# Down-projection of a conv-FFN layer with its operand sums on VectorE, output work in smaller pieces over more steps, samples' sums copied out at its start, and TensorE's last feature tile written in program order

## The chip, the cores and the metric

One core of a Trainium2 chip (trn2). The metric is the device time of one execution in microseconds (us). The kernel before took 1695.22 us, the median of three runs (1693.51 to 1695.83).

## What is computed

One layer of a chunk-causal streaming encoder on a prompt of 1024 rows and 8 sample sequences of 16 rows, all in float32. Token mixing (attention and spatial gating) comes first; the change touches only the second half, the channel mixing:

```python
D_MODEL = 1024; SEQ = 1024; DEC_BATCH = 8; DEC_SEQ = 16; CONV_W = 3; D_FF = 2816

def conv_ffn(h, conv_cache, w_ffn_in, ffn_conv_w, ffn_conv_b, w_ffn_out):
    g, u = jnp.split(h @ w_ffn_in, 2, axis=-1)
    gp = jnp.concatenate([conv_cache, g], axis=1)
    gc = ffn_conv_b
    for j in range(CONV_W):
        gc = gc + ffn_conv_w[j] * gp[:, j:j + T]
    out = (jax.nn.gelu(gc) * u) @ w_ffn_out
    return out, gp[:, -(CONV_W - 1):]

x = x + gt2 * conv_ffn(h2, ...)[0]      # gt2: a gate, one row for the prompt, one for each sample
```

The last two rows of gp of every sequence are outputs as well (the conv rows).

## The kernel before

A float32 matrix product is made of three matmuls: each operand is split into a rounded part and the rest (`split`, lines 77 and 78: ScalarE, called ACT, copies the rounded part, VectorE, called DVE, subtracts it), and rounded x rounded, rounded x rest and rest x rounded are added up in PSUM. Large products are made by Strassen's scheme, seven products of half-size blocks in place of eight; their operands are blocks (A11, A12, A22 and so on) and sums of blocks (S1 to S4 of the activations, T1 to T4 of the weights).

**Feature tiles (lines 1074 to 1337, loop at 1542).** The 2816 features are 22 tiles, f = 0 to 21. Of each, `up_weights` loads four blocks of w_ffn_in (SyncE, called SP, issues the loads), GpSimd (POOL) makes t3, t1, t2 and t4 out of them (lines 1093, 1094, 1098, 1102), and ACT and DVE split them into wB11, wB21, wT2, wT1, wT3, wT4, wB22. `unit(f, u)` makes the tile in two halves, u = 0 and 1, each of seven products (`product`, matmul at line 1225) of twelve matmuls, 128 x 288 each: X takes A11, then S2 with T2, S3 with T3 and A22 with T4; Y takes A12; Z takes S1 with T1 and S4 with B22. Between its products X is copied out by ACT: x1c at line 1301, u2 at 1315 (after T2), u3 at 1321 (after T3), and the last at 1331. The next product into X waits for the copy. Convolution, GELU and gate follow on ACT and DVE, and `gated` stores the gated tile to DRAM (aT_d, line 1269). `sample_down(f, hf)` does the samples' part of the down-projection at once: three matmuls (line 1283) add to acc_s, two PSUM banks held from f = 0 to the end. It also makes sums of w_ffn_out blocks on POOL and stores them for later.

**Down-projection (`down`, line 1375, and its inner functions).** Seven products (j = 0 to 6, `KINDS`) of eleven steps k, 77 steps n. A step is twelve matmuls, 128 x 512 each (`multiply`, line 1495), into four banks dX or dZ. `prepare(j, k)` runs three steps ahead: it loads the blocks of activations (`load_a`, line 1394, tiles named ar) and of weights (`get`, line 1406; dB, dT and, for T3, a second one dT3y), makes a sum of two (T3 at 1422, S1 at 1429, S2 at 1431, S3 at 1433, S4 at 1435) and splits both into da and dw. `finish` takes a full bank out, and `delay(n, ...)` puts its further work (add to another bank's, times the gate g2p, plus x1, store) some steps later. `scaled` (line 1453) loads the x1 rows and does the gate's product and the sum on POOL. `samples_out` (line 1499) reads acc_s at step 9, `conv_rows` (line 1355) at step 10 transposes the conv rows on PE (glt, line 1359), copies them (glo, DVE, line 1361) and stores them in five pieces (SP, lines 1365 to 1369). The gates are loaded at steps 1 and 2 (g2p, line 1522) and 1 to 8 (g2s, 16 small loads, line 1526).

**What sets the order.** Every engine, SP's DMA queue too, works through its own list in order; an instruction at the head that has to wait holds up all behind it. For f = 0 the order on PE, ACT and DVE is that of the code (`by_hand`). For f from 1 on a scheduler sets it. In `down` the order of all five engines is again that of the code.

Of the kernel before, what the change touches and what calls it, by code (L numbers as in the profile page):

```python
# [9 lines left out]
F32 = mybir.dt.float32  # L10
# [28 lines left out]
def tile_layer(ctx: ExitStack, tc: tile.TileContext, io):  # L39
# [838 lines left out]
    def staged(name, n=512):  # L878
        return wst.tile([P, 512], F32, tag="wst", name=name)[:, :n]
# [495 lines left out]
    def down():  # L1375
# [28 lines left out]
        def get(src, nm, second=False):  # L1404
            t = dn.tile([P, 512], F32, tag="sub", name=nm, bufs=3) if second else staged(nm)
            sp.dma_start(t, src)
            return t

        def prepare(j, k):
# [8 lines left out]
            if B[0] == "B":  # L1418
                t = get(weight_rows(B[1:], k), f"d{B}_{k}")
            elif B == "T3":  # L1420
                t, t2 = get(weight_rows("22", k), f"dT3_{k}"), get(weight_rows("12", k), f"dT3y_{k}", True)
                pool.tensor_tensor(t, t, t2, ALU.subtract)
            else:
                t = get({"T1": t1_d, "T2": t2_d, "T4": t4_d}[B][k], f"d{B}_{k}")
# [3 lines left out]
            if j == 1:  # L1428
                pool.tensor_tensor(bs1, b21, b22, ALU.add)
            if j == 2:  # L1430
                dve.tensor_tensor(b11, bs1, b11, ALU.subtract)
            if j == 3:
                pool.tensor_tensor(b21, b22, b11, ALU.subtract)
            if j == 5:
# [5 lines left out]
        def x1_rows(t, hf):  # L1440
            r = dn.tile([P, 512], F32, tag="x1r", name=f"x1r{t}_{hf}", bufs=3)
            sp.dma_start(r, x1_d[t * P:(t + 1) * P, 512 * hf:512 * (hf + 1)])
            return r
# [8 lines left out]

        def scaled(y, t, hf, out, mult=True):
            r = x1_rows(t, hf)
            if mult:
                pool.tensor_tensor(y, y, g2p[:, 512 * hf:512 * (hf + 1)], ALU.mult)
            pool.tensor_tensor(y, y, r, ALU.add)
            if out:
                delay(2, lambda: sp.dma_start(y_rows(t)[:, 512 * hf:512 * (hf + 1)], y))

        at = [0]

        def finish(j, i):

            lo, hi = slice(0, 512), slice(512, 1024)
            c, u = keep("c", i), keep("u", i)
            if j == 0:
                act.activation(c, X[i], AF.Copy)
            if j == 1:
                delay(1 + 2 * i, lambda: dve.tensor_tensor(c, Z[i], c, ALU.add))  # L1470
                delay(12 + 2 * i, lambda: scaled(c, i, 0, True))
            if j == 2:
                act.activation(u, X[i], AF.Copy)
                delay(12 + 2 * i, lambda: scaled(u, i, 1, False))
            if j == 4:
                act.activation(c, X[i], AF.Copy)
                delay(1 + 2 * i, lambda: dve.tensor_tensor(c, Z[i], c, ALU.add))
                delay(2 + 2 * i, lambda: scaled(c, i + 4, 1, True))
            if j == 5:
                delay(1 + i, lambda: dve.tensor_tensor(c, X[i], g2p[:, lo], ALU.mult))  # L1480
                delay(2 + i, lambda: scaled(c, i + 4, 0, True, False))
            if j == 6:
# [16 lines left out]
        def samples_out():  # L1499
            for hf in range(2):  # L1500
                cs = slice(512 * hf, 512 * (hf + 1))
                r, y = x1_rows(NTP, hf), keep("u", hf)
                dve.tensor_tensor(y, acc_s[hf], g2s[:, cs], ALU.mult)
                dve.tensor_tensor(y, y, r, ALU.add)
                delay(2, lambda y=y, cs=cs: sp.dma_start(y_rows(NTP)[:, cs], y))

# [5 lines left out]
        with tc.manual_schedule(engines={e.engine for e in (pe, act, dve, pool, sp)}):  # L1512
            for n, (j, k) in enumerate(steps[:-TAIL]):
# [5 lines left out]
                for i in range(4):  # L1519
                    multiply(j, k, i)  # L1520
                if n in (1, 2):
                    sp.dma_start(g2p[:, 512 * (n - 1):512 * n], dap(ada_d, (2 * P + 32 * (1 + n)) * 512, [[0, P], [1, 512]]))
                if 1 <= n < 9:
                    for x in range(2 * n - 2, 2 * n):
                        hf, b = divmod(x, DB)
                        sp.dma_start(g2s[DS * b:DS * (b + 1), 512 * hf:512 * (hf + 1)], dap(ada_d, (2 * P + 32 * (2 + hf) + 1 + b) * 512, [[0, DS], [1, 512]]))
                if n == 9:
                    samples_out()
                if n == 10:
                    conv_rows()  # L1530
                for e in [e for e in waiting if e[0] <= n]:
# [10 lines left out]
    prev = None  # L1542
    for f in range(NF):
        nxt = ws[f + 1] if f + 1 < NF else iter(())
        for u in range(2):
            plain = (f, u) == (0, 1)
            g = plain_unit(f, u, W[f]) if plain else unit(f, u, W[f])
            for i in range(8 if plain else 5):
# [3 lines left out]
                if f == 0:  # L1552
                    next(pair1)
                    if (u, i) == (0, 0):
                        later.pop()[1]()
                    if u == 0:
                        next(ws[0], None)
                if u == 1 and i > 0 if f == 0 else u == 1 or i >= 3:
                    next(nxt, None)
                if f and u == 1 and i >= 3:  # L1560
                    sample_down(f - 1, i - 3)
            prev = None if plain else g
# [6 lines left out]
    for hf in range(2):  # L1569
        sample_down(NF - 1, hf)  # L1570
    ffn.close()
    down()


# [25 lines left out]
```

## Time and profile before

| | |
|---|---|
| runs | 1693.51, 1695.22, 1695.83 us, median 1695.22 |
| profiled execution | 1697.72 us, its span 1696.0 us |
| TensorE (PE) busy | 1629.7 us, 96% of the span, 10668 matmuls |
| DVE, ACT, POOL busy | 976.4 (58%), 740.4 (44%), 483.7 us (29%) |
| mean DMA | 123 GB/s over the span |

The feature tiles end in the profile at about 1442 us, the down-projection fills the rest. In rows of the profile, "L1495 PE MATMUL dX<-dw,da" is line, engine, operation and output<-inputs; "x528" counts instructions. In the timeline a row is a run of like instructions: start, duration, what, and in brackets how long the engine was idle before, and what ended that. In the list of waits a row names the waiting engine with its output and line, behind the arrow who was waited for with output and line, and then the total in us, how often, and the longest. SPq is SP's DMA queue.

### The profile page before, as it was taken

What the parts mean: (1) busy time and instruction counts of PE and PEld (TensorE: products, weight loads), DVE (VectorE), ACT (ScalarE), POOL (GpSimd) and SP (SyncE); (2) the same over time, 40 slices, a digit from 0 to 9 for tenths busy, and PEclk for the clock granted to TensorE, in tenths of its full rate; (3) what the DMA queues carried; (4) which work ended last, traced back from release to release, by engine and by line L of the source; (5) the groups of instructions that cost most, each with busy time, mean ns of one, the idle gap of its engine ahead of it and who ended that gap; (6) DMA issues with size and microseconds to landing.
All of it is one profiled execution on the core that took longest, in us unless ns stands there. A gap on an engine that the chain in (4) does not pass through costs nothing.

```text
span 1696.0 us, 28728 instructions
## 1 busy us (share of the span) xinstructions
PE 1629.7 (96%) x10668; PEld 1475.9 (87%) x10668; DVE 976.4 (58%) x2028; ACT 740.4 (44%) x1613; POOL 483.7 (29%) x591
## 2 busy tenths in 40 slices
PE   6999999999999999999997999999999999879998
PEld 5799888799998989999876999999999999657787
DVE  4552111127657643465467866666676776457997
ACT  5442111126655543553245555555554545334443
POOL 5510000025324310023211233332444344033852
PEclk9999999999999999999998999999999999899999
DMA  9114444531110133274531233333333434683644
GB/s 354 66 61 160 152 128 137 171 90 34 50 29 25 25 108 108 86 238 144 170 110 60 84 99 106 94 101 105 105 115 119 126 110 146 203 277 102 215 139 147
DMA packets 170689, 207.79 MB, mean 123 GB/s; under 512 B 14648, under 2 KB 117028, under 8 KB 170549
## 3 DMA queue, kind: packets, MB, share of 16 engines
q1 hardware_dynamic: 170549, 205.96, 37.9%
q8 instruction: 84, 1.38, 0.3%
q14 instruction: 56, 0.46, 0.1%
HBM read 163.19 MB, written 44.78 MB: 123 GB/s over the span
## 4 chain that ended last, share of the span: by engine, by line
PE 76%; DVE 7%; DMA 6%; issue 3%; ACT 3%; POOL 2%; SPq 1%; POOLq 0%; ACTq 0%; DVEq 0%
PE X L1225 13%; PE Z L1225 6%; PE dX L1495 4%; PE mxps L1179 4%; PE Y L1225 3%; PE dZ L1495 3%; PE o L692 2%; DMA dB<-in_w_ffn_out_dram 2%; PE qkps L101 2%; PE qkps L103 2%; PE qkps L102 2%; PE gaps L101 2%; PE gaps L102 2%; PE gaps L103 2%; PE gbps L103 2%
## 5 line engine op out<-in xcount | busy, mean ns | idle before, releaser
L1225 PE MATMUL X<-op,wT 128*128 128x288 f32 x1200 | 189.4, 298 | 11.0 <-ACT u L1321 8.5
L1225 PEld LDWEIGHTS X<-op,wT 128*128 128x128 f32 x1200 | 171.9, 190 | 15.2 <-ACT u L1321 10.6
L1495 PE MATMUL dX<-dw,da 128*128 128x512 f32 x528 | 126.9, 398 | 7.6 <-ACT da L77 7.2
L1495 PEld LDWEIGHTS dX<-dw,da 128*128 128x128 f32 x528 | 99.8, 191 | 33.4 <-ACT da L77 9.5
L1179 PE MATMUL mxps<-wo,mT 128*128 128x512 f32 x432 | 104.4, 396 | 0.3 <-DVE wo L78 0.2
L1495 PE MATMUL dZ<-dw,da 128*128 128x512 f32 x396 | 95.8, 399 | 5.2 <-ACT da L77 2.7
L1495 PEld LDWEIGHTS dZ<-dw,da 128*128 128x128 f32 x396 | 75.2, 192 | 25.0 <-DVE da L78 6.0
L1179 PEld LDWEIGHTS mxps<-wo,mT 128*128 128x128 f32 x432 | 79.8, 189 | 17.4 <-DVE wo L78 1.0
L101 PE MATMUL qkps<-wqk,h1T 128*128 128x256 f32 x288 | 83.5, 290 | 0.8 <-ACT qf L586 0.8
L102 PE MATMUL qkps<-wqk,h1T 128*128 128x256 f32 x288 | 81.9, 284 | 0.0
L103 PE MATMUL qkps<-wqk,h1T 128*128 128x256 f32 x288 | 81.8, 284 | 0.0
L1225 PE MATMUL Z<-opS1h,wT 128*128 128x288 f32 x344 | 79.0, 295 | 0.0
L1093 POOL TENSOR_TENSOR t<-b,b 128x512 f32<-128x512 f32 x22 | 35.5, 1612 | 144.1 <-DMA b<-in_w_ffn_in_dram 144.1
L78 DVE TENSOR_TENSOR da<-ar,da 128x512 fp32r<-128x512 f32 x66 | 68.0, 1031 | 14.6 <-ACT da L77 14.6
L78 DVE TENSOR_TENSOR wsm<-ws,wsm 128x512 fp32r<-128x512 f32 x44 | 30.4, 690 | 72.8 <-ACT wsm L77 72.8
L78 DVE TENSOR_TENSOR wT<-t,wT 128x512 fp32r<-128x512 f32 x44 | 40.9, 929 | 52.7 <-ACT wT L77 52.7
L1257 ACT ACTIVATE gc<-gp,parT 128x288 f32<-128x288 f32 (+2 forms) x110 | 59.3, 574 | 21.2 <-DVE gp L1309 14.6
L636 POOL MEMSET ql<- 128x256 f32 x2 | 0.6, 320 | 236.3 <-PE adaps L386 236.3
L101 PE MATMUL gaps<-h1T,wga 128*128 128x384 f32 x192 | 66.5, 346 | 0.0
L1260 ACT ACTIVATE gc<-gc 128x288 f32<-128x288 f32 x88 | 38.8, 440 | 62.6 <-DVE gc L1259 62.6
L103 PE MATMUL gbps<-h1T,wgb 128*128 128x384 f32 x192 | 65.9, 343 | 0.0
L102 PE MATMUL gaps<-h1T,wga 128*128 128x384 f32 x192 | 65.0, 339 | 0.0
(484 smaller groups left out, 4846.2 us busy)
## 6 DMA issues: line engine op xcount, KB each, us to landing
adaw<-in_w_ada_dram SPq DMA_DIRECT2D x48, 512.0 KB, 6.2
b<-in_w_ffn_in_dram SPq DMA_DIRECT2D x88, 256.0 KB, 3.1
ws<-in_w_ffn_out_dram SPq DMA_DIRECT2D x44, 256.0 KB, 2.8
ar<-aT_d SPq DMA_DIRECT2D x44, 256.0 KB, 5.8
aT_d<-gc SPq DMA_DIRECT2D x66, 144.0 KB, 1.8
dB<-in_w_ffn_out_dram SPq DMA_DIRECT2D x33, 256.0 KB, 4.7
dT<-t_d SPq DMA_DIRECT2D x33, 256.0 KB, 2.7
t_d<-ws SPq DMA_DIRECT2D x22, 256.0 KB, 2.1
```

Source lines behind the costliest of these rows:

```text
L78: (eng or dve).tensor_tensor(lo, src, hi.bitcast(F32), ALU.subtract)
L101: pe.matmul(ps, lhsT=ah, rhs=bh, start=(i == 0), stop=False)
L102: pe.matmul(ps, lhsT=ah, rhs=bl, start=False, stop=False)
L103: pe.matmul(ps, lhsT=al, rhs=bh, start=False, stop=(i == n - 1))
L636: pool.memset(ql.bitcast(F32), 0.0)
L692: pe.matmul(o[hs, :], lhsT=v[:, k0 // P + i, hs], rhs=out[t, x][:, i * P:(i + 1) * P], start=(i == 0), stop=(i == nk - 1))
L1093: pool.tensor_tensor(t3, b22, b12, ALU.subtract)
L1179: pe.matmul(ps, lhsT=a[:, k, o:o + P], rhs=w[:, b, :], start=(k == n == 0), stop=(k == KD - 1 and n == 2))
L1225: pe.matmul(ps, lhsT=w[:, wj, ks], rhs=x, start=(begin and n == 0), stop=(n == 11), skip_group_check=True)
L1257: act.activation(g, a0, AF.Identity, bias=bb, scale=w0)
L1260: act.activation(gc, gc, AF.Gelu_apprx_tanh)
L1495: pe.matmul(ps, lhsT=a[:, x, o], rhs=w[:, y, :], start=(j in (0, 1, 3) and k == n == 0), stop=(k == NK - 1 and n == 2), skip_group_check=True)
```

## The change

- In `prepare` the sums T3, S1 and S3 go from POOL to DVE (S2 and S4 are there already). The tiles of the second load (tag sub) are two in place of three, those of the x1 rows four in place of three.
- `scaled` is cut in two, `times_gate` and `plus_x1`, with the engine as an argument, and each is put at a step of its own. Only the four products and four sums on u (j = 2) stay on POOL; those of c and of the new v (the blocks of S1, free by then) go to DVE.
- acc_s is copied to SBUF by ACT at step 0; `samples_out` moves from step 9 to 24, `conv_rows` from step 10 to 3; the gate loads from steps 1 to 8 to steps 12 to 19.
- In the feature loop PE's order is that of the code from f = 21 on, and the sample part of tile f - 1 is called in the first half of tile f (for f > 1) in place of the second.

```diff
-            t = dn.tile([P, 512], F32, tag="sub", name=nm, bufs=3) if second else staged(nm)
+            t = dn.tile([P, 512], F32, tag="sub", name=nm, bufs=2) if second else staged(nm)
...
-                pool.tensor_tensor(t, t, t2, ALU.subtract)
+                dve.tensor_tensor(t, t, t2, ALU.subtract)
...
-                pool.tensor_tensor(bs1, b21, b22, ALU.add)
+                dve.tensor_tensor(bs1, b21, b22, ALU.add)
...
-                pool.tensor_tensor(b21, b22, b11, ALU.subtract)
+                dve.tensor_tensor(b21, b22, b11, ALU.subtract)
...
-        def scaled(y, t, hf, out, mult=True):
+        def times_gate(y, hf, eng):
+            eng.tensor_tensor(y, y, g2p[:, 512 * hf:512 * (hf + 1)], ALU.mult)
+
+        def plus_x1(y, t, hf, out, eng):
             r = x1_rows(t, hf)
-            if mult:
-                pool.tensor_tensor(y, y, g2p[:, 512 * hf:512 * (hf + 1)], ALU.mult)
-            pool.tensor_tensor(y, y, r, ALU.add)
+            delay(2, lambda: eng.tensor_tensor(y, y, r, ALU.add))
             if out:
-                delay(2, lambda: sp.dma_start(y_rows(t)[:, 512 * hf:512 * (hf + 1)], y))
+                delay(4, lambda: sp.dma_start(y_rows(t)[:, 512 * hf:512 * (hf + 1)], y))
...
             if j == 1:
                 delay(1 + 2 * i, lambda: dve.tensor_tensor(c, Z[i], c, ALU.add))
-                delay(12 + 2 * i, lambda: scaled(c, i, 0, True))
+                delay(12 + 2 * i, lambda: times_gate(c, 0, dve))
+                delay(21 + 2 * i, lambda: plus_x1(c, i, 0, True, dve))
             if j == 2:
                 act.activation(u, X[i], AF.Copy)
-                delay(12 + 2 * i, lambda: scaled(u, i, 1, False))
+                delay(28 + 2 * i, lambda: times_gate(u, 1, pool))
+                delay(27 + 2 * i, lambda: plus_x1(u, i, 1, False, pool))
             if j == 4:
-                act.activation(c, X[i], AF.Copy)
-                delay(1 + 2 * i, lambda: dve.tensor_tensor(c, Z[i], c, ALU.add))
-                delay(2 + 2 * i, lambda: scaled(c, i + 4, 1, True))
+                act.activation(v, X[i], AF.Copy)
+                delay(1 + 2 * i, lambda: dve.tensor_tensor(v, Z[i], v, ALU.add))
+                delay(11 + i, lambda: times_gate(v, 1, dve))
+                delay(10 + i, lambda: plus_x1(v, i + 4, 1, True, dve))
             if j == 5:
-                delay(1 + i, lambda: dve.tensor_tensor(c, X[i], g2p[:, lo], ALU.mult))
-                delay(2 + i, lambda: scaled(c, i + 4, 0, True, False))
+                delay(2 + i, lambda: dve.tensor_tensor(c, X[i], g2p[:, lo], ALU.mult))
+                delay(2 + i, lambda: plus_x1(c, i + 4, 0, True, dve))
...
-                if n in (1, 2):
+                if n in (12, 13):
...
-                if 1 <= n < 9:
+                if 12 <= n < 20:
...
-                if n == 9:
+                if n == 0:
+                    for hf in range(2):
+                        act.activation(keep("u", hf), acc_s[hf], AF.Copy)
+                if n == 3:
+                    conv_rows()
+                if n == 24:
                     samples_out()
-                if n == 10:
-                    conv_rows()
...
     for f in range(NF):
+        if f == NF - 1:
+            by_hand.enter_context(tc.manual_schedule(engines={pe.engine}))
...
+                if f > 1 and u == 0 and i in (2, 3):
+                    sample_down(f - 1, i - 2)
...
-                if f and u == 1 and i >= 3:
-                    sample_down(f - 1, i - 3)
+                if f == 1 and u == 1 and i >= 3:
+                    sample_down(0, i - 3)
```

In the changed kernel the matmul of `multiply` is line 1499; lines up to 1452 keep their numbers.

PE where the last feature tile goes over into the down-projection, before (X21_1 is the second half's X, its operand after the arrow names the weights; dX0 to dX3 are the down-projection's banks, dw0_1 and da0_1 the operands of j = 0, k = 1):

```order
L1225 MATMUL X21_1_15821<-op112_9555,wT2_21_15580 128x288
L1495 MATMUL dX0_16075<-dw0_0_16051,da0_0_16054 128x512 x2
L1225 MATMUL X21_1_15821<-op112_9555,wT3_21_15639 128x288 x12
L1495 MATMUL dX0_16075<-dw0_0_16051,da0_0_16054 128x512
L1495 MATMUL dX1_16076<-dw0_0_16051,da0_0_16054 128x512 x3
L1495 MATMUL dX2_16077<-dw0_0_16051,da0_0_16054 128x512 x3
L1495 MATMUL dX3_16078<-dw0_0_16051,da0_0_16054 128x512 x3
L1495 MATMUL dX0_16075<-dw0_1_16060,da0_1_16063 128x512
L1283 MATMUL sm0_10018<-wsm21_0_16002,as21_15894 128x512 x2
L1283 MATMUL sm1_10046<-wsm21_1_16010,as21_15894 128x512 x2
L1495 MATMUL dX0_16075<-dw0_1_16060,da0_1_16063 128x512
L1225 MATMUL X21_1_15821<-op102_9554,wT4_21_15654 128x288 x12
```

And now:

```order
L1225 MATMUL Z21_1_15847<-opS1h1_9726,wT1_21_15643 128x288
L1499 MATMUL dX0_16078<-dw0_0_16054,da0_0_16057 128x512 x3
L1499 MATMUL dX1_16079<-dw0_0_16054,da0_0_16057 128x512 x3
L1499 MATMUL dX2_16080<-dw0_0_16054,da0_0_16057 128x512 x3
L1499 MATMUL dX3_16081<-dw0_0_16054,da0_0_16057 128x512 x3
L1225 MATMUL X21_1_15845<-op112_9555,wT3_21_15661 128x288 x12
L1499 MATMUL dX0_16078<-dw0_1_16063,da0_1_16066 128x512 x3
L1499 MATMUL dX1_16079<-dw0_1_16063,da0_1_16066 128x512 x3
L1499 MATMUL dX2_16080<-dw0_1_16063,da0_1_16066 128x512 x3
L1499 MATMUL dX3_16081<-dw0_1_16063,da0_1_16066 128x512 x3
L1499 MATMUL dX0_16078<-dw0_2_16072,da0_2_16075 128x512 x2
L1225 MATMUL X21_1_15845<-op102_9554,wT4_21_15676 128x288 x12
```

Before, two matmuls of the first dX step stood ahead of the T3 product of tile 21 and the rest of that step behind it. Now the first step stands whole behind the S1 product of the second half (Z21_1 with wT1_21), which in the old list came earlier than these rows, and two whole steps stand ahead of the T4 product.

ACT in the middle of the feature tiles, tile 16 going over into 17, before (wT2_17 is a weight sum from POOL being split, u316_0 the copy of X at line 1321, x1c the copy at 1301):

```order
L77 ACTIVATE wB21_17_14337<-b17_10_14314 128x512
L1315 ACTIVATE u216_0_14296<-X16_0_14203 128x288
L1260 ACTIVATE gc15_3_14236<-gc15_3_14236 128x288
L1260 ACTIVATE gc16_0_14261<-gc16_0_14261 128x288
L77 ACTIVATE wT2_17_14384<-t2_17_14382 128x512
L77 ACTIVATE wT1_17_14425<-b17_01_14312 128x512
L1321 ACTIVATE u316_0_14333<-X16_0_14203 128x288
L77 ACTIVATE wT3_17_14443<-t3_17_14340 128x512
L1301 ACTIVATE x1c16_1_14358<-X16_1_14343 128x288
```

And now:

```order
L1315 ACTIVATE u216_0_14296<-X16_0_14203 128x288
L77 ACTIVATE wB21_17_14359<-b17_10_14336 128x512
L1260 ACTIVATE gc15_3_14236<-gc15_3_14236 128x288
L1260 ACTIVATE gc16_0_14261<-gc16_0_14261 128x288
L1321 ACTIVATE u316_0_14355<-X16_0_14203 128x288
L1301 ACTIVATE x1c16_1_14380<-X16_1_14365 128x288
L77 ACTIVATE wT2_17_14406<-t2_17_14404 128x512
L77 ACTIVATE wT1_17_14447<-b17_01_14334 128x512
L77 ACTIVATE wT3_17_14465<-t3_17_14362 128x512
```

The copy u3 at line 1321 stood behind wT2_17 and wT1_17; now it and x1c stand ahead of them.

SP around the conv rows' stores (o_cp and o_cs), before:

```order
L1394 DMA ar21_16037<-aT_d21_110 128x512
L1394 DMA ar00_16028<-aT_d2_91 128x512
L1394 DMA ar20_16032<-aT_d13_102 128x512
L1406 DMA dB21_2_16334<-in_w_ffn_out_dram 128x512
L1365 DMA o_cp_dram<-glo_16364 44x128
L1366 DMA o_cs_dram<-glo_16364 84x128
L1369 DMA o_cs_dram<-glo_16364 128x128 x2
L1369 DMA o_cs_dram<-glo_16364 12x128
L1394 DMA ar01_16029<-aT_d3_92 128x512
L1394 DMA ar20_16032<-aT_d14_103 128x512
L1406 DMA dB21_3_16373<-in_w_ffn_out_dram 128x512
```

And now:

```order
L1394 DMA ar10_16033<-aT_d6_95 128x512
L1394 DMA ar20_16035<-aT_d14_103 128x512
L1269 DMA aT_d21_110<-gc21_2_15899 128x288
L1269 DMA aT_d21_110<-gc21_3_15980 128x288
L1406 DMA dB11_6_16154<-in_w_ffn_out_dram 128x512
L1365 DMA o_cp_dram<-glo_16179 44x128
L1366 DMA o_cs_dram<-glo_16179 84x128
L1369 DMA o_cs_dram<-glo_16179 128x128 x2
L1369 DMA o_cs_dram<-glo_16179 12x128
L1394 DMA ar10_16033<-aT_d7_96 128x512
L1394 DMA ar21_16036<-aT_d15_104 128x512
L1406 DMA dB11_7_16188<-in_w_ffn_out_dram 128x512
```

The five stores stood between the loads of j = 1, k = 2 and k = 3; now they stand between those of j = 0, k = 6 and k = 7, with two stores of the last gated tile (aT_d) close ahead of them.

More of the change, by code (lines that the diff above doesn't have):

```diff
@@ L1440, in x1_rows @@
         def x1_rows(t, hf):
-            r = dn.tile([P, 512], F32, tag="x1r", name=f"x1r{t}_{hf}", bufs=3)
+            r = dn.tile([P, 512], F32, tag="x1r", name=f"x1r{t}_{hf}", bufs=4)
             sp.dma_start(r, x1_d[t * P:(t + 1) * P, 512 * hf:512 * (hf + 1)])
@@ L1465, in finish @@
             lo, hi = slice(0, 512), slice(512, 1024)
-            c, u = keep("c", i), keep("u", i)
+            c, u, v = keep("c", i), keep("u", i), block("S1", i)
             if j == 0:
@@ L1502, in samples_out @@
                 r, y = x1_rows(NTP, hf), keep("u", hf)
-                dve.tensor_tensor(y, acc_s[hf], g2s[:, cs], ALU.mult)
-                dve.tensor_tensor(y, y, r, ALU.add)
-                delay(2, lambda y=y, cs=cs: sp.dma_start(y_rows(NTP)[:, cs], y))
+                dve.tensor_tensor(y, y, g2s[:, cs], ALU.mult)
+                delay(1, lambda y=y, r=r: dve.tensor_tensor(y, y, r, ALU.add))
+                delay(3, lambda y=y, cs=cs: sp.dma_start(y_rows(NTP)[:, cs], y))
         steps = [(j, k) for j in range(len(KINDS)) for k in range(NK)]
@@ L1520, in down @@
                     multiply(j, k, i)
-                if n in (1, 2):
-                    sp.dma_start(g2p[:, 512 * (n - 1):512 * n], dap(ada_d, (2 * P + 32 * (1 + n)) * 512, [[0, P], [1, 512]]))
-                if 1 <= n < 9:
-                    for x in range(2 * n - 2, 2 * n):
+                if n in (12, 13):
+                    sp.dma_start(g2p[:, 512 * (n - 12):512 * (n - 11)], dap(ada_d, (2 * P + 32 * (n - 10)) * 512, [[0, P], [1, 512]]))
+                if 12 <= n < 20:
+                    for x in range(2 * n - 24, 2 * n - 22):
                         hf, b = divmod(x, DB)
                         sp.dma_start(g2s[DS * b:DS * (b + 1), 512 * hf:512 * (hf + 1)], dap(ada_d, (2 * P + 32 * (2 + hf) + 1 + b) * 512, [[0, DS], [1, 512]]))
-                if n == 9:
+                if n == 0:
[4 more added lines that the diff above has]
+                if n == 24:
                     samples_out()
-                if n == 10:
-                    conv_rows()
                 for e in [e for e in waiting if e[0] <= n]:
@@ L1570, in tile_layer @@
         sample_down(NF - 1, hf)
+    by_hand.close()
     ffn.close()
```

## Prediction

> **What bounds the kernel now.** The page first. The profiled execution took 1697.72 us, 1.72 outside its span.
>
> ```profile
> span 1696.0 us, 28728 instructions
> L1495 PE MATMUL dX<-dw,da 128*128 128x512 f32 x528 | 126.9, 398 | 7.6 <-ACT da L77 7.2
> L1495 PE MATMUL dZ<-dw,da 128*128 128x512 f32 x396 | 95.8, 399 | 5.2 <-ACT da L77 2.7
> ar<-aT_d SPq DMA_DIRECT2D x44, 256.0 KB, 5.8
> dB<-in_w_ffn_out_dram SPq DMA_DIRECT2D x33, 256.0 KB, 4.7
> ```
>
> The two matmul groups of the down-projection are TensorE's (PE's), with little idle time before them (7.6 and 5.2 us), so a gain has to come out of the few places where PE waits or runs slowly; ar and dB are their loads, 5.8 and 4.7 us to land. The change touches two stages, the feature tiles (up to 1442 us) and the down-projection behind them. The down-projection has 528 + 396 = 924 matmuls, 12 to a step, 77 steps. The waits of PE from 1440 us on:
>
> ```profile
> PE dX L1495 <- ACT da L77: 7.2, 2, 4.6
> PE glt L1359 <- DVE u L1503: 5.9, 1, 5.9
> PE dZ L1495 <- ACT da L77: 2.7, 2, 2.3
> PE dZ L1495 <- DVE da L78: 2.3, 6, 0.4
> PE dX L1495 <- DVE da L78: 0.2, 1, 0.2
> ```
>
> Together 18.3 us, 12.4 of them over operands (da) that came late and 5.9 over the samples' output. PE's timeline shows where (start, duration, count, idle before):
>
> ```profile
> 1447.37 1.22 PE L1495 MATMUL dX<-dw,da 128*128 128x512 f32 x2 [4.58 <-ACT da L77]
> 1448.52 3.25 PE L1225 MATMUL X<-op,wT 128*128 128x288 f32 x12
> ...
> 1472.77 19.82 PE L1495 MATMUL dX<-dw,da 128*128 128x512 f32 x72 [2.65 <-ACT da L77]
> 1498.44 1.11 PE L1359 MATMUL glt<-ident,glast 128*128 128x128 f32 x4 [5.85 <-DVE u L1503]
> 1499.20 10.67 PE L1495 MATMUL dZ<-dw,da 128*128 128x512 f32 x36
> 1512.18 3.37 PE L1495 MATMUL dZ<-dw,da 128*128 128x512 f32 x12 [2.31 <-ACT da L77]
> ```
>
> The chain that ended last shows the same matmuls unhindered:
>
> ```profile
> 1601.67 59.89 PE dX L1495 x264
> 1661.57 29.93 PE dZ L1495 x132
> ```
>
> That is 59.89/264 = 0.2269 us each, 2.72 a step. A product of the feature tiles, twelve matmuls of 288 columns, takes 12 x 40.00/296 = 1.6 us by this row of the windows view (length, PE busy and count first):
>
> ```profile
> 1000.00:1040.00 40.00, 40.00 (x296) 39.59 (x295) 24.22 (x52) 21.23 (x47) 12.32 (x16) 1.00 0.32 98
> 1240.00:1420.00 180.00, 173.74 (x1261) 170.17 (x1262) 125.09 (x249) 89.08 (x200) 73.47 (x74) 1.00 0.37 118
> ```
>
> From the start of the first wait (1447.37 - 4.58 = 1442.79) to PE's last matmul (1661.57 + 29.93 = 1691.50) pass 248.7 us. Work in it: 924 x 0.2269 = 209.6, three products of the last feature 4.8, six sample matmuls 1.4, transposes 0.8; sum 216.6. **32.1 us are lost**: 18.3 waiting, 13.8 in matmuls slower than their rate (the twelve at 1448.52 take 3.25 for 1.6, the 72 at 1472.77 take 19.82 for 16.3, the 36 at 1499.20 take 10.67 for 8.2). From 1601.67 on nothing is lost; the 4.5 us behind the last matmul are a tail that the change leaves.
>
> In the feature tiles the windows above show PE full at 1000 and 180.00 - 173.74 = 6.3 us idle from 1240 to 1420.
>
> **Part 1: ScalarE's order in the feature tiles.** PE's largest wait before 1440 us, and ScalarE (ACT) at one of its nine places:
>
> ```profile
> PE X L1225 <- ACT u L1321: 8.5, 9, 1.7
> PE X L1225 <- ACT u L1315: 2.5, 1, 2.5
> ```
>
> ```profile
> 1387.68 0.63 ACT L77 ACTIVATE wT<-t 128x512 fp32r<-128x512 f32 x1 [2.44 <-POOL t L1098]
> 1388.22 0.61 ACT L77 ACTIVATE wT<-b 128x512 fp32r<-128x512 f32 x1
> 1388.74 0.39 ACT L1321 ACTIVATE u<-X 128x288 f32<-128x288 f32 x1
> ```
>
> The copy of X at L1321, for which PE's next product waits, stands in ACT's queue behind two weight splits (L77), the first of which waits 2.44 us for GpSimd (POOL). In the changed order it stands ahead of both, so POOL no longer delays PE. The other operands of a feature keep at least 1 us by the order, counting 1.6 us a product. Eight of the nine waits lie after 1240, about 6.8 us of the 8.5: I take **-6.8**, bounds 0 (another operand is then late) and -8.5.
>
> The samples' product of a feature moves to the first half of the next one, same matmuls, nothing added. Against this, around feature 20's second half the order puts the T3 and T4 products right behind T2's into the same X, with no product between: T3 waits for the copy at L1315, T4 for L1321, each 0.39 us (last row) plus the hand-over. The nearest rows bound two such waits by 0 below and 2.5 + 1.7 = 4.2 above; I take 0.6 + 0.9 = **+1.5**, nearer the low end, as nothing else is queued ahead of the copies.
>
> **Part 2: the start of the down-projection.** Before, the first two dX matmuls stand on PE's queue ahead of product T3 of the last feature and wait 4.58 us for their operand; then the rest follows at a low clock. In the changed order the load's block comes free with the last feature's second A11 product, and five products (T4, A12, S4, S2, S1) stand between that and the first dX: 8.0 us of work, against 5.8 to land and 1.3 for its two splits (0.63 on ACT, row above, 0.68 on DVE, rows of part 3). The 4.58 goes, with 0.9 us to spare. What is late next? SyncE (SP), which issues all loads in order:
>
> ```profile
> SPq L1394 <- PE X L1225: 7.8, 1, 7.8
> SPq L1365 <- DVE glo L1361: 7.6, 1, 7.6
> ...
> 1494.09 0.38 SPq L1406 DMA_DIRECT2D dB<-in_w_ffn_out_dram  x1
> 1502.75 0.32 SPq L1365 DMA_DIRECT2D o_cp_dram<-glo  x1
> 1503.11 0.35 SPq L1366 DMA_DIRECT2D o_cs_dram<-glo  x1
> 1503.51 1.50 SPq L1369 DMA_DIRECT2D o_cs_dram<-glo  x3
> 1505.06 0.91 SPq L1394 DMA_DIRECT2D ar<-aT_d  x2
> ```
>
> Twice SP stood still for over 7 us with loads queued behind: for the last feature's T4, and for the conv rows' copy (glo). The loads of step 14 went out at 1505.06 instead of 1494.5 and PE starved at 1512.18, 7.1 us later. Both the conv rows (now step 3) and the sixteen small gate loads (now steps 12 to 19) move on this queue. Moving the gate loads leaves 3 DMAs a step in place of 5 (0.45 us each, as two take 0.91: 1.4 in place of 2.3) while the lead is smallest; at steps 12 to 19 they have some 3 us of lead by the same count, so they are hidden. Copying the samples' sums at step 0 removes the 5.85 us at 1498.44: that product then waits for nothing.
>
> But glo now stands earlier on SP. Counting from the end T of the last feature's T4: SP issues ten DMAs at 0.45, done at T+4.5, and stops at glo. The last of them is step 6's weights, landing at T+9.2; its split on ACT (0.6) and four DVE operations, the copy the last of them, follow (2.4): glo ready T+12.2, five stores of 2.3 us as above, loads of step 7 out at T+14.5, the second of them 0.45 behind, landed (5.8) and split (1.3) at T+22. PE meanwhile: S4 1.6, sample matmuls 1.4, the rest of step 2 2.3, step 3 2.7, transposes 0.8, steps 4 to 6 8.2: T+17.0. **A wait of about 5 us before step 7 remains.** Cover gone entirely, 8 us (SP's 7.6 again); best case, with the stores out of the way early, 0.
>
> After a wait PE also runs slowly. The granted clock (third column from the end) after those waits:
>
> ```profile
> 1470.00:1480.00 10.00, 7.30 (x23) 5.19 (x23) 2.59 (x4) 2.85 (x6) 0.00 (x0) 0.83 0.92 305
> 1500.00:1510.00 10.00, 9.87 (x35) 7.58 (x34) 2.72 (x4) 2.72 (x6) 0.84 (x2) 0.80 0.42 120
> ```
>
> The 5.85 us cost 10.67 - 8.2 = 2.5 more, the 2.65 us cost 19.82 - 16.3 = 3.5. I take 2.5. So of the 32.1 us 7.5 remain: **-24.6**, bounds -32.1 and, with the wait at 8 and the clock at 3.5 and another such step as at 1512.18 (2.3 + 0.7), -17.6.
>
> [...]
>
> **Part 3: sums from POOL to DVE.** DVE's pace beside POOL's last sum of block T3 and right behind it, with the start of each:
>
> ```profile
> 1623.51 1.78 DVE L78 TENSOR_TENSOR dw<-dT,dw 128x512 fp32r<-128x512 f32 x1
> 1625.21 0.68 DVE L78 TENSOR_TENSOR da<-ar,da 128x512 fp32r<-128x512 f32 x1
> 1625.82 0.68 DVE L78 TENSOR_TENSOR dw<-dT,dw 128x512 fp32r<-128x512 f32 x1
> ```
>
> Beside POOL the next operation starts 1.70 later, alone 0.61. Now 154 splits, 55 sums and 47 output operations, 256 in all, come to 156 us, and the eight operations left on POOL add 8 x 1.1 = 9: 165 us under 210 of PE. The densest block (T3, j = 4) has three to four a step, 2.5 under 2.72. Zero cost, hidden under PE; its gain, the seven waits for DVE (2.5 us), is already in part 2. With two sub buffers dT3y's load goes out two steps ahead, 5.4 us for some 4 of load; if that cover fails, 1 us a step, +11.
>
> **Sum.** 1697.72 - 6.8 + 1.5 - 24.6 = 1667.8 against the profiled execution, which stood 2.5 above the median of 1695.22; against the median 1665.3. Forecast 1665.
>
> **Rivals.** (a) The samples' matmuls become PE's wait: they now come 11 products earlier in the next feature than before, behind loads of 2.8 us, an ACT split (0.6) and a DVE split (0.7).
>
> ```profile
> ws<-in_w_ffn_out_dram SPq DMA_DIRECT2D x44, 256.0 KB, 2.8
> ```
>
> If the load goes out only one product (1.6) ahead, each of some 20 features waits 2.8 + 1.3 - 1.6 = 2.5 us: +50, 1715, **slower**. It decides from about 30/20 = 1.5 us a feature. Against it: by the order the last that they wait for is a DVE split that is released two products (3.2 us) ahead of them and takes 0.7 with some 1.5 queued before it. 5%. (b) The feature tiles keep their waits (the copy at L1321 goes first, but T2's weights from POOL are then what X waits for): +6.8, 1672. For: POOL's sums are in the same chain; against: the order leaves them over 1 us. 12%. (c) Loads stay the limit at the start: glo on SP costs 8, a second starved step follows: +7, 1672; with DVE late in block T3, +11, 1676. For: SP stood still twice, 7.8 and 7.6. 15%. (d) No wait at step 7 and none at the turn of features: -7.5 - 1.5, 1656. 8%. (e) The change does nothing for PE, since a wait removed at the start of the down-projection comes back behind it: 1695. Against: from 1601 on nothing is late. 3%. The forecast itself 57%.
>
> **Numbers.** The range 1655 to 1680 holds the forecast, (b), (c) and (d), with the ends of parts 1 and 2. What a measurement of this kernel tells from no change is 0.2%, 3.4 us. Faster 0.91, within 0.2% 0.03, slower 0.06 ((a), and one in a hundred for what no row shows).
>
> **What would show it.** Right: no waits for L1321 after 1240; the first dX matmul with no idle before it; one wait of about 5 us some seven steps into the down-projection, on the operand behind glo's stores, then none to the end; DVE at 0.68 in block T3. Wrong: waits on sm or on L1315 in every feature, several starved steps, or DVE rows at 1.78 without POOL.

## The result, and the profile after

The changed kernel took 1670.05 us, the median of four runs (1668.54 to 1673.52), against 1694.37 for the kernel before (four runs, 1692.45 to 1695.83): a ratio of 0.986, 95% interval 0.9841 to 0.9879. That is 24.3 us faster, where 29.9 were forecast (1695.2 to 1665.3). The profiled execution took 1670.79 us with a span of 1669.0. Its span is 27.0 us shorter than that of the profile before, and 2.7 of these lie ahead of anything that was changed: the first product into Y, at the beginning of the feature tiles, starts at 904.64 us in place of 907.36. The rest, 24.3, is the gain.

Beginning with the feature tiles, the windows view (length, then PE busy) and PE's waits from 1240 us to the end:

```profile
1240.00:1400.00 160.00, 160.00 (x1171) 158.07 (x1171) 110.47 (x235) 83.81 (x184) 61.58 (x66) 1.00 0.40 126
```

```profile
PE dX L1499 <- ACT da L77: 5.3, 2, 4.7
PE dZ L1499 <- ACT da L77: 0.6, 1, 0.6
PE X L1225 <- ACT u L1321: 0.5, 1, 0.5
PE X L1225 <- ACT u L1315: 0.5, 1, 0.5
PE dZ L1499 <- DVE dw L78: 0.2, 1, 0.2
```

From 1240 to 1400 us PE is never idle; the eight waits for the copy at line 1321 are gone. The two waits of 0.5 us are the ones at the turn of tile 20. Of 18.3 us of waits in the down-projection 6.1 are left. PE's timeline shows them (start, duration, count, idle before):

```profile
1433.97 2.93 PE L1499 MATMUL dX<-dw,da 128*128 128x512 f32 x12
1438.33 3.35 PE L1499 MATMUL dX<-dw,da 128*128 128x512 f32 x14
...
1451.45 8.46 PE L1499 MATMUL dX<-dw,da 128*128 128x512 f32 x36
1464.66 13.58 PE L1499 MATMUL dX<-dw,da 128*128 128x512 f32 x48 [4.75 <-ACT da L77]
1478.08 30.08 PE L1499 MATMUL dZ<-dw,da 128*128 128x512 f32 x132
1507.99 19.30 PE L1499 MATMUL dX<-dw,da 128*128 128x512 f32 x84
1527.87 12.53 PE L1499 MATMUL dX<-dw,da 128*128 128x512 f32 x48 [0.57 <-ACT da L77]
1540.23 30.08 PE L1499 MATMUL dZ<-dw,da 128*128 128x512 f32 x132
1570.15 60.00 PE L1499 MATMUL dX<-dw,da 128*128 128x512 f32 x264
1629.99 21.02 PE L1499 MATMUL dZ<-dw,da 128*128 128x512 f32 x90
1651.65 1.84 PE L1499 MATMUL dZ<-dw,da 128*128 128x512 f32 x4 [0.64 <-ACT da L77]
1653.67 10.83 PE L1499 MATMUL dZ<-dw,da 128*128 128x512 f32 x38 [0.17 <-DVE dw L78]
```

The first dX step has no idle time before it. Seven products are seven stretches here; their lengths, from one product's first matmul to the next one's, tell where time is lost better than the waits do. (The row of 264 matmuls is two of them, j = 4 and 5.) An unhindered product takes 132 x 0.2267 = 29.92 us (1540.23 to 1570.15); the first, with four small pieces of the feature tiles in it, takes 36.66 at best and the last 30.08 to the modelled end of its last matmul (experiments below). The changed kernel loses 7.4 in the first product (44.11), 2.3 in the third, j = 2 (32.24), and 4.4 in the last (34.51): 14.2 us where the prediction left 7.5.

The first loss is SP's. Its DMA queue around the conv rows' stores:

```profile
1447.74 0.56 SPq L1406 DMA_DIRECT2D dB<-in_w_ffn_out_dram  x1
1455.99 0.32 SPq L1365 DMA_DIRECT2D o_cp_dram<-glo  x1
1456.36 0.35 SPq L1366 DMA_DIRECT2D o_cs_dram<-glo  x1
1456.77 1.27 SPq L1369 DMA_DIRECT2D o_cs_dram<-glo  x3
1458.08 0.81 SPq L1394 DMA_DIRECT2D ar<-aT_d  x2
```

T, the end of the last feature's T4 product, is 1443.27 here. The stores began at T+12.7 (forecast 12.2), step 7's loads went out at T+14.8 (14.5), and PE waited 4.75 us (5). The granted clock in the window behind it was 0.66 (third column from the end):

```profile
1460.00:1470.00 10.00, 5.34 (x13) 4.09 (x14) 2.92 (x5) 3.29 (x6) 0.00 (x0) 0.66 0.97 320
```

and 48 matmuls took 13.58 us instead of 10.89, 2.7 more.

### The profile page after: what moved, and what is told of

Its sections match the earlier page's. It is cut to its first block, busy times and chain, and to the rows that moved or that the text cites. A ratio compares the mean times of both kernels' runs of the same rounds, so it can differ in the third digit from the quotient of the medians.

```text
span 1669.0 us, 28648 instructions
## 1 busy us (share of the span) xinstructions
PE 1621.8 (97%) x10668; PEld 1474.4 (88%) x10668; DVE 948.4 (57%) x2081; ACT 741.7 (44%) x1615; POOL 409.5 (25%) x538
## 4 chain that ended last, share of the span: by engine, by line
PE 80%; DVE 7%; DMA 6%; ACT 3%; issue 3%; SPq 1%; POOL 1%; ACTq 0%; DVEq 0%; POOLq 0%
PE X L1225 15%; PE Z L1225 7%; PE dX L1499 5%; PE Y L1225 4%; PE mxps L1179 3%; PE dZ L1499 3%; PE o L692 2%; PE gbps L103 2%; PE qkps L101 2%; PE gbps L101 2%; PE gbps L102 2%; PE qkps L103 2%; PE qkps L102 2%; PE gaps L101 2%; PE gaps L102 2%
## 5 line engine op out<-in xcount | busy, mean ns | idle before, releaser
L101 PE MATMUL gaps<-h1T,wga 128*128 128x384 f32 x192 | 66.6, 347 | 0.0
L103 PE MATMUL gbps<-h1T,wgb 128*128 128x384 f32 x192 | 65.9, 343 | 0.0
L102 PE MATMUL gaps<-h1T,wga 128*128 128x384 f32 x192 | 65.2, 340 | 0.0
L101 PE MATMUL gbps<-h1T,wgb 128*128 128x384 f32 x192 | 64.9, 338 | 0.0
L102 PE MATMUL gbps<-h1T,wgb 128*128 128x384 f32 x192 | 64.7, 337 | 0.0
L103 PE MATMUL gaps<-h1T,wga 128*128 128x384 f32 x192 | 64.3, 339 | 0.0
L77 ACT ACTIVATE da<-ar 128x512 fp32r<-128x512 f32 x66 | 41.2, 624 | 46.1 <-DVE ar L1431 22.2
```

The source lines that it names most:

```text
L77: act.activation(hi, src, AF.Copy)
L101: pe.matmul(ps, lhsT=ah, rhs=bh, start=(i == 0), stop=False)
L102: pe.matmul(ps, lhsT=ah, rhs=bl, start=False, stop=False)
L103: pe.matmul(ps, lhsT=al, rhs=bh, start=False, stop=(i == n - 1))
```

## The experiments

The median of the kernel before lies between 1691.53 and 1696.55 us on the chips used, so times of runs on different chips are not compared by themselves; the ratio to the kernel before on the same chip stands with each (with its 95% interval), and the length of the products from the profiles. The theory that they started from: what the change gained, it gained by the order in which ACT and SP work; what is still lost is lost where SP stands at a store or at a tile that is not free, with loads queued behind. Rivals: the gain comes from taking sums away from POOL; the loads' rate is the limit; DVE is the limit.

**The changed loop alone, and the changed down-projection alone.** The first takes `down` from before, the second the feature loop.

```diff
+        if f == NF - 1:
+            by_hand.enter_context(tc.manual_schedule(engines={pe.engine}))
...
+                if f > 1 and u == 0 and i in (2, 3):
+                    sample_down(f - 1, i - 2)
...
-                if f and u == 1 and i >= 3:
-                    sample_down(f - 1, i - 3)
+                if f == 1 and u == 1 and i >= 3:
+                    sample_down(0, i - 3)
...
+    by_hand.close()
```

e1 is the kernel before with these lines, e2 the changed kernel without them.

> The down-projection of before with only the changed feature loop (samples' part in the first half of the next tile, PE in program order from f = 21). Theory (PE's waits in the feature tiles and the wait of the first dX step go through the order alone): the eight waits for the copy at line 1321 after 1240 us go (-7.1), the turn at tile 20 costs +1.0, the 4.58 us before the first dX and the slow matmuls right behind it go (-4.6 - 2), the rest of the down-projection keeps its waits: about 1694.4 - 12.7 = 1681.7. Rival (an earlier start only lengthens the wait at the next late load): -6 only, 1688.

> The changed down-projection behind the feature loop of before. Theory: the feature tiles keep their 6.8 us of waits for line 1321, the first dX step its 4.58; what the down-projection gains behind that is the rest, 24.3 - 12.7 = 11.6: about 1682.8. Rival (the two parts overlap, SP's wait for the conv rows' copy takes what the loop saves): the sum of both parts' gains is clearly more than 24.3, this one alone gives -18, 1676.

Measured 1679.49 (ratio 0.9913, 0.9887 to 0.9938) and 1680.98 (0.9925, 0.9898 to 0.9952). The gains are 0.87% and 0.75%, together 1.62% where the whole change gives 1.40%; the intervals allow that they simply add. Both came within 2.5 us of the theory. In e1 no wait for line 1321 is left but one of 0.5 us, and the first dX has no wait; in e2 seven waits for line 1321 (5.3 us) and the wait before the first dX are there:

```profile
1443.04 1.22 PE L1499 MATMUL dX<-dw,da 128*128 128x512 f32 x2 [4.36 <-ACT da L77]
...
1473.06 3.38 PE L1499 MATMUL dX<-dw,da 128*128 128x512 f32 x12 [1.69 <-ACT da L77]
```

The second row is e2's step 7: where PE starts late, it waits 1.69 there in place of 4.75. So part of what the loop gains at the start is paid back at the conv rows' stores: some 3 us in this profile, an overlap that the times are too noisy to show.

**The sums on POOL again.**

```diff
-                dve.tensor_tensor(t, t, t2, ALU.subtract)
+                pool.tensor_tensor(t, t, t2, ALU.subtract)
...
-                dve.tensor_tensor(bs1, b21, b22, ALU.add)
+                pool.tensor_tensor(bs1, b21, b22, ALU.add)
...
-                dve.tensor_tensor(b21, b22, b11, ALU.subtract)
+                pool.tensor_tensor(b21, b22, b11, ALU.subtract)
```

> The changed kernel with the three sums T3, S1, S3 on GpSimd again, all else as changed. Theory (SP's order and the start made the gain, DVE had slack): DVE is slowed beside POOL, but only block T3 is too dense for it; the seven waits of 0.2 to 0.4 us come back, +2 to +4, 1672 to 1674. Rival (the sums' move is what made the gain): +8 or more, 1678 or later, with DVE waits all through j = 1, 3 and 4.

Measured 1673.97 (0.9888, 0.9865 to 0.9912), 4 us above the changed kernel in the medians, 4.7 by the ratios, whose intervals overlap. The size is the theory's, the place is not: block T3 (j = 4) kept its rate, 59.83 us for the two products, and the waits came in j = 2, which took 37.51 in place of 32.24. There the splits of da take 1.13 to 1.15 us beside POOL's sums:

```profile
1519.04 0.68 DVE L1431 TENSOR_TENSOR ar<-ar_s,ar 128x512 f32<-128x512 f32 x1
1520.50 1.15 DVE L78 TENSOR_TENSOR da<-ar,da 128x512 fp32r<-128x512 f32 x1 [0.78 <-ACT da L77]
```

So the sums' move is worth some 4 us of the 24 by the times; in the profiles j = 2 takes 5.3 more, but from the first dX to the end it is only 1.9 (232.4 against 230.5), as the waits at step 7 and in the last product are shorter here. Why j = 2 should be the tender place was open at this point.

**The conv rows' stores five steps later**, their copy in a tile that is not in use yet.

```diff
-    def conv_rows():
+    def conv_rows(glo, later):
...
-        glo = staged("glo").rearrange("p (i n) -> p i n", i=4)
+        glo = glo.rearrange("p (i n) -> p i n", i=4)
...
+        def store():
+            sp.dma_start(cp, glo[0:n0, 0, :])
...
+        later(store)
...
-                    conv_rows()
+                    conv_rows(keep("u", 2), lambda do: delay(5, do))
```

> The changed kernel with the conv rows' copy in a tile of its own (the third of u, not yet in use) and its five stores five steps later, so that SP never stands at them. Theory (the 4.75 us wait at step 7 and the slow matmuls behind it come from SP standing at the stores): both go, -7.3, 1662.8. Rival (the loads' rate is the limit at the start, 3 x 256 KB a step): a wait of 2 us or more remains among steps 5 to 12, -3, 1667.

Measured 1662.31 (0.9817, 0.9795 to 0.9839). The wait at step 7 is gone, and the first product takes 36.66 us in place of 44.11:

```profile
1452.02 19.34 PE L1503 MATMUL dX<-dw,da 128*128 128x512 f32 x84
1471.19 30.08 PE L1503 MATMUL dZ<-dw,da 128*128 128x512 f32 x132
1501.11 16.68 PE L1503 MATMUL dX<-dw,da 128*128 128x512 f32 x72
1518.93 3.30 PE L1503 MATMUL dX<-dw,da 128*128 128x512 f32 x12 [1.14 <-ACT da L77]
1522.81 12.53 PE L1503 MATMUL dX<-dw,da 128*128 128x512 f32 x48 [0.58 <-ACT da L77]
```

From the first dX to the end PE takes 223.1 us in place of 230.5. That settles step 7: SP standing at the stores, not the loads' rate. The copy's tile was changed in the same edit, but in the changed kernel SP waited there for the copy:

```profile
SPq L1365 <- DVE glo L1361: 7.2, 1, 7.2
```

But j = 2 now takes 34.07, 1.8 more than in the changed kernel: what was late there had been covered by PE's own delay. (In e7 below PE loses most ahead of this block, and there j = 2 takes 29.92.)

**The samples' stores later as well**, on top of e4. In the changed kernel SP's longest wait in the down-projection was for the data of these stores (total, count, longest):

```profile
SPq L1509 <- DVE u L1508: 13.0, 2, 12.8
```

```diff
-                delay(3, lambda y=y, cs=cs: sp.dma_start(y_rows(NTP)[:, cs], y))
+                delay(6, lambda y=y, cs=cs: sp.dma_start(y_rows(NTP)[:, cs], y))
```

> As e4_glo_late, and the two stores of the samples' rows at step 30 in place of 27. Theory: the waits around step 29 (1.14 and 0.58 us there, and slow matmuls behind them, about 3.5 in all) come from SP standing 12.8 us at these stores while the weights of the next steps queue behind: they go, -3, 1659.3. Rival (they come from DVE, which has the samples' products and sums ahead of the splits there): the waits stay, 1662.

Measured 1666.70 (0.9826, 0.9807 to 0.9845), no gain: the waits are still 1.08 and 0.58 us, j = 2 takes 34.41. SP stands at most 2.3 us at these stores now, and nothing else changed. The theory fell here: SP's 12.8 us at the samples' stores had cost nothing.

**The x1 rows of the last pieces out of the ring** (the four tiles of tag x1r, used in turn), and the stores of the prompt's rows three steps later, on top of e5.

```diff
-        def x1_rows(t, hf):
-            r = dn.tile([P, 512], F32, tag="x1r", name=f"x1r{t}_{hf}", bufs=4)
+        def x1_rows(t, hf, r=None):
+            if r is None:
+                r = dn.tile([P, 512], F32, tag="x1r", name=f"x1r{t}_{hf}", bufs=4)
...
-                delay(4, lambda: sp.dma_start(y_rows(t)[:, 512 * hf:512 * (hf + 1)], y))
+                delay(7, lambda: sp.dma_start(y_rows(t)[:, 512 * hf:512 * (hf + 1)], y))
...
-                delay(10 + i, lambda: plus_x1(v, i + 4, 1, True, dve))
+                delay(10 + i, lambda: plus_x1(v, i + 4, 1, True, dve, block("21", i)))
...
-                delay(2 + i, lambda: plus_x1(c, i + 4, 0, True, dve))
+                delay(2 + i, lambda: plus_x1(c, i + 4, 0, True, dve, block("21", i + 4)))
```

> As e5_samples_late, and the x1 rows of the last eight output pieces go to blocks of the activations that are free by then, not to the ring of four, and all stores of the prompt's rows three steps later. Theory: SP stands 9.4 us at a ring tile in product 6's loads; with that gone the waits in the last product go (0.64 + 0.17 and slow matmuls, about 4 us in all): 1655.5, and PE runs from the first dX step to the end without a wait over 0.1 us. Rival (the end is bound by DVE, which has its densest output work there): the waits stay, 1659.

Measured 1662.64 (0.9801, 0.978 to 0.9821). The last product takes 30.08 us in place of 32.52 (e5) and has no wait, 2.4 us gained where some 4 were expected; j = 2 is unchanged at 34.50. In the changed kernel, where the last product takes 34.51, SP stood here, in a row of two loads that took it 9.38 us, since a ring tile was still to be read by DVE; the last product's weights left behind it:

```profile
1623.29 0.33 SPq L1406 DMA_DIRECT2D dB<-in_w_ffn_out_dram  x1
1623.72 9.38 SPq L1442 DMA_DIRECT2D x1r<-x_d  x2
1633.19 0.38 SPq L1406 DMA_DIRECT2D dB<-in_w_ffn_out_dram  x1
```

The ring had been made four in place of three; that was not enough for loads whose sums come steps later. The two edits of this kernel (tiles and store steps) were not tried apart.

**The gate loads at steps 1 to 8 again.**

```diff
-                if n in (12, 13):
+                if n in (1, 2):
...
-                if 12 <= n < 20:
+                if 1 <= n < 9:
```

> The changed kernel with the gate loads at steps 1 to 8 again, all else as changed. Theory (18 more issues of 0.45 us on SP while the loads' lead is smallest): the wait at step 7 grows, since two steps' gate loads stand ahead of the conv rows' stores and the rest behind them among the loads; +3 to +5, 1674. Rival (the loads wait for the stores anyway, the gate loads fit into SP's idle time): same, 1670.

Measured 1674.37 (0.9873, 0.9848 to 0.9898). In the profile there are two waits, 3.63 and 3.82 us, in the first product and three more up to 0.99 in the second; from the first dX to the end it takes 235.0 us against 230.5, +4.5. By the ratios it is +2.2, inside both intervals, so the size rests on one profile.

**The conv rows at step 10 again.**

```diff
-                if n == 3:
+                if n == 10:
                     conv_rows()
```

> The changed kernel with the conv rows at step 10 again, all else as changed. Theory (SP stands at the stores wherever their copy is ordered just before them, since SP's list is some five steps ahead of PE): from the end of step 10, transposes 0.4, copy 0.9, stores 2.3, load 0.9 + 5.8, splits 1.3 make 11.6 against three steps of work, 8.2: a wait of about 3.4 us at step 14 in place of 4.75 at step 7; -1.5, 1668.5. Rival (the earlier place is what helped): a wait of 5.9 us or more at step 10 to 14, 1672 or later.

Measured 1669.85 (0.9851, 0.983 to 0.9873): the same as at step 3. The wait is 1.98 us at step 14 and 0.67 behind it, and the second product takes 35.41 in place of 29.91, while the first takes 36.5. The move from step 10 to step 3 by itself bought nothing; the rival (the earlier place helped) falls, and the expected gain of 1.5 is too small to see.

**The sums ahead of the weights' split.** What is late in j = 2? DVE's timeline in the changed kernel (start, duration, idle before):

```profile
1508.80 0.68 DVE L78 TENSOR_TENSOR dw<-dT,dw 128x512 fp32r<-128x512 f32 x1
1509.40 0.69 DVE L1431 TENSOR_TENSOR ar<-ar_s,ar 128x512 f32<-128x512 f32 x1
1510.87 0.69 DVE L78 TENSOR_TENSOR da<-ar,da 128x512 fp32r<-128x512 f32 x1 [0.78 <-ACT da L77]
1511.47 0.68 DVE L78 TENSOR_TENSOR dw<-dT,dw 128x512 fp32r<-128x512 f32 x1
```

Three operations a step, 0.6 us apart where nothing holds them, but one step to the next is 2.67 (1508.80 to 1511.47): the split of da needs ACT's copy of the sum that DVE has just made, and DVE idles 0.78 us for it. PE takes 2.72. There is 0.05 us to spare, and eight operations of output work stand in this block at 0.6 each. The kernel before has the same step there, since the sum S2 was DVE's already:

```profile
1556.54 0.68 DVE L78 TENSOR_TENSOR dw<-dT,dw 128x512 fp32r<-128x512 f32 x1
1557.14 0.69 DVE L1431 TENSOR_TENSOR ar<-ar_s,ar 128x512 f32<-128x512 f32 x1
1558.60 0.69 DVE L78 TENSOR_TENSOR da<-ar,da 128x512 fp32r<-128x512 f32 x1 [0.78 <-ACT da L77]
1559.21 0.68 DVE L78 TENSOR_TENSOR dw<-dT,dw 128x512 fp32r<-128x512 f32 x1
```

Beside POOL's sums it is 3.13 there, and the kernel before took 31.78 us for j = 2. Four of the eight output operations are the samples', which the change moved into this block (step 24); no run has them elsewhere. The edit makes the sum first, so that ACT's copy runs while DVE splits dw; it was made to the best kernel so far and, alone, to the changed one.

```diff
+            if j == 2:
+                dve.tensor_tensor(b11, bs1, b11, ALU.subtract)
+            if j == 5:
+                dve.tensor_tensor(b12, b12, b11, ALU.subtract)
             w = wp.tile([P, 2, 512], F32R, tag="w", name=f"dw{j}_{k}")
             split(w[:, 0, :], w[:, 1, :], t)
...
-            if j == 2:
-                dve.tensor_tensor(b11, bs1, b11, ALU.subtract)
...
-            if j == 5:
-                dve.tensor_tensor(b12, b12, b11, ALU.subtract)
```

> As e6_all_late, and in prepare the sums S2 and S4 stand ahead of the weights' split in place of behind it. New theory (the waits of 1.06 and 0.56 us in block j = 2 are DVE's: each step is dw split, sum, 0.78 us idle for ACT's copy of that sum, da split = 2.68 us against PE's 2.72, so the four samples' and the output operations there cannot be caught up): with the sum first, ACT copies while DVE splits dw, the cycle falls to about 1.9, both waits and the slow matmuls of the block go: the 4.6 us that j = 2 takes beyond 29.9, to 1658.0 on a chip where e6 took 1662.6. Rival (the loads of T2 are late there): j = 2 stays at 34.5.

> The changed kernel with only the sums S2 and S4 ahead of the weights' split. Theory: block j = 2 takes 29.9 in place of 32.2, -2.3; the wait at step 7 (4.75) and those of the last product stay: about 1667.7. Rival: no change, 1670.

Measured 1656.75 (0.9786, 0.9765 to 0.9807) and 1664.79 (0.9831, 0.981 to 0.9852). DVE's step and idle time with the edit, in e9:

```profile
1500.25 0.68 DVE L78 TENSOR_TENSOR dw<-dT,dw 128x512 fp32r<-128x512 f32 x1
1501.12 0.69 DVE L78 TENSOR_TENSOR da<-ar,da 128x512 fp32r<-128x512 f32 x1 [0.18 <-ACT da L77]
1501.72 0.69 DVE L1431 TENSOR_TENSOR ar<-ar_s,ar 128x512 f32<-128x512 f32 x1
1502.33 0.68 DVE L78 TENSOR_TENSOR dw<-dT,dw 128x512 fp32r<-128x512 f32 x1
```

The step is 2.08 us now, and j = 2 takes 29.92 in both kernels. The new theory holds for this block. In e10 the wait at step 7 (3.62) and those of the last product stay, as expected; by the ratios it gains 4.9 us on the changed kernel, intervals overlapping, and 2.3 of them are j = 2's. In e9 PE runs from the first dX to the end without a wait:

```profile
1468.37 30.08 PE L1504 MATMUL dZ<-dw,da 128*128 128x512 f32 x132
1498.29 30.08 PE L1504 MATMUL dX<-dw,da 128*128 128x512 f32 x132
1528.21 30.08 PE L1504 MATMUL dZ<-dw,da 128*128 128x512 f32 x132
...
1617.97 30.08 PE L1504 MATMUL dZ<-dw,da 128*128 128x512 f32 x132
```

From the first dX to the end e9 takes 216.3 us, e6 221.2. The ratios of these two (0.9786 and 0.9801) do not tell them apart, so that step of 4.8 us rests on the profiles. e9 is 2.1% faster than the kernel before, and on the ratios 0.75% faster than the changed one.

**PE scheduled to the end of the feature tiles, and the samples' part in the second half again.**

```diff
 e11_pe_scheduled:
-        if f == NF - 1:
-            by_hand.enter_context(tc.manual_schedule(engines={pe.engine}))
...
 e12_samples_second_half:
-                if f > 1 and u == 0 and i in (2, 3):
-                    sample_down(f - 1, i - 2)
...
-                if f == 1 and u == 1 and i >= 3:
-                    sample_down(0, i - 3)
+                if f and u == 1 and i >= 3:
+                    sample_down(f - 1, i - 3)
```

> The changed kernel without PE's program order from f = 21 on (samples' part still in the first half of the next tile). Theory (two edits of the loop, two gains): ACT's order in the feature tiles stays the changed one, so no waits for line 1321 there; the first dX matmuls stand ahead of tile 21's T3 product again and wait some 4.4 us, with slow matmuls behind (2); the two waits at the turn (0.5 each) go: +5.5, 1675.5. Rival (the wait only moves: what PE waits there it waits less at step 7): +1, 1671.

> The changed kernel with the samples' part in the second half of the next tile again (PE's program order from f = 21 on stays). Theory: ACT has the copy of line 1321 behind two weight splits again, the eight waits come back: +7, 1677, and no 4.58 us before the first dX. Rival (the waits go for another reason): same, 1670.

Measured 1668.13 (0.9861, 0.9831 to 0.989) and 1674.24 (0.989, 0.9869 to 0.991). PE's program order is worth nothing that can be measured here: without it the first dX waits 1.18 us, not 4.4, and the two waits at the turn are gone. The theory for e11 was wrong. In e11 PE reached the first dX 4.0 us after SP had issued the first of its loads, in the kernel before 1.25 us after; why SP was earlier was not followed up. The samples' place is worth 3 per mille, about 5 us (the intervals just overlap): with it back, the waits for line 1321 are eight again, 5.6 us:

```profile
PE X L1225 <- ACT u L1321: 5.6, 8, 1.4
```

and, as in e2, PE's later start takes some of it back (the wait at step 7 is 1.02). The first dX has no wait in e12.

## Why the prediction was right, and where it was not

- **Part 1, ACT's order: right.** -6.8 forecast; the 6.8 us of waits after 1240 are gone, and e12 brings 5.6 of them back by the samples' place alone. What moved ACT's order was that edit, though the diff names the samples.
- **The turn at tile 20: right in kind and place**, 1.0 us of waits for a forecast of 1.5.
- **Part 2, the start: right.** No wait before the first dX; SP stood at the conv rows' copy and PE waited 4.75 us at step 7, with 2.7 us of slow matmuls: 7.4 where 7.5 were forecast. e4 takes away the standing and with it all 7.4. That the figures meet so closely is partly luck: e3 and e10, the same kernel up to there, wait 3.6 us. The first dX wait goes by PE's program order alone (e12), but nearly all of it goes by the samples' place alone, too (1.18 us left in e11); neither edit is the one cause.
- **The clock behind the wait.** The profile's row gave 2.5 us; 2.7 were measured, and 2.8 behind the 3.62 us wait of e10 (13.73 for 48 matmuls). In windows of 1 us the changed kernel's granted clock is 0.52 from 1463 us on, while PE still waits, 0.50 up to 1469, 0.57 behind that and 1.00 from 1470: by estimate 2.6 us lost in 5.2 us of PE's work. Not all slow matmuls are the clock's, as the prediction took them to be: behind the 2.65 us wait of the kernel before the same windows (0.64, 0.50, 0.50, 0.65 from 1473 us) account, by estimate, for 1.7 of the 3.5 us, and in j = 2 of the changed kernel 48 matmuls took 12.53 us in place of 10.89 with the granted clock at 1.00 throughout. Behind e12's wait of 1.02 us it stayed at 1.00 as well.
- **Part 3, DVE hidden under PE at zero cost: this step failed, but not by the sums that moved.** "165 us under 210" compared DVE's busy time with PE's. In j = 2 DVE's list, not its work, sets the pace: 1.9 us of work and 0.78 of idle time in a step of 2.67. That step is older than the change, and moving the other sums off POOL made it shorter (e3), not longer; the prediction's sum left nothing of the 1.9 us that the kernel before lost in j = 2. What stayed was 2.3 us in the changed kernel, 4.6 once e4 to e6 had taken away the delay that covered it. The densest block was expected at T3, where DVE does not lag at all and two sub buffers were enough (60.00 us for two products).
- **"Then none to the end": this failed too.** The x1 rows' ring is named in the change, and nothing was worked out for it: SP's two loads there took 9.38 us before the last product, which lost 4.4 us in this profile (2.4 in e5's; e6 takes that away). Part of it is the clock's, which fell to 0.50 at 1655 us though no wait there was longer than 0.64.
- **The sum.** 2.3 + 4.4 = 6.7 us of loss were not foreseen, 0.5 were foreseen at the turn and did not come: 6.2, against 29.9 - 24.3 = 5.6 missed; the rest is within the spread of the runs. 1670.05 lies nearer to the 1672 of (b) and (c) than to 1665, but no rival's mechanism came true: (a), the early samples' matmuls never wait in the changed kernel; (b), of the waits in the feature tiles only the two at the turn are left, 1.0 us; (c) named late loads and DVE in T3, but the lateness was in j = 2 and at the x1 ring.

## What to carry to other kernels

An engine's slack is not its idle share: where it hands a result to another engine and needs the answer back within the same step, the round trip counts (in j = 2 DVE's 0.78 us of idle time in a step of 2.67), so order its list so that independent work stands between, and take a step's length from the starts of like instructions. In a queue that works in order, ask of each store and each load into a ring how many steps lie between it and the instruction that makes its data or frees its tile; SP stood 12.8 us at one store at no cost and 7.2 at another for 7.4 us, and only removing each tells which. Two losses in a row can hide each other (j = 2 went from 32.24 to 34.07 us when e4 took the 7.4 ahead of it away), so measure by stretches of equal work, not by waits.

## What the runs showed that was not expected

In the changed kernel one POOL product of two tiles in SBUF took 17.41 us. It began while DVE's list had no gap:

```profile
1540.78 17.41 POOL L1454 TENSOR_TENSOR u<-u,g2p 128x512 f32<-128x512 f32 x1 [110.48 <-DVE ar L1433]
```

```profile
1556.35 0.69 DVE L1433 TENSOR_TENSOR ar<-ar,ar 128x512 f32<-128x512 f32 x1
1557.42 1.32 DVE L78 TENSOR_TENSOR da<-ar_s,da 128x512 fp32r<-128x512 f32 x1 [0.39 <-ACT da L77]
```

The other three products of its line took 1.73 to 1.75. Beside the long one DVE's two-input operations ran at 0.68 or 0.69, one behind another, up to DVE's first gap, 0.39 us; it ended behind that gap, and the next DVE operation took 1.32. A profile's spans on POOL are rough, but there is a second such row in the same trace: the sum at line 1458 that began at 1609.24 us took 4.85, beside DVE operations of 0.68 without a gap, where the other three sums of that line took 1.30 to 1.64. In the kernel before, with POOL operations one behind another from 1599.20 to 1624.74 us, it was DVE that took 1.77 or 1.78 for each. So POOL is the slow one in some places of these traces and DVE in others; what decides which was not shown. Here nothing waited for the long product.
